# Up products of tile pairs by seven half-width products, with ScalarE's copies of sums into a second PSUM bank

## The chip, the cores and the metric

The kernel runs on one core of a Trainium2 chip. The metric is the device time of one execution in microseconds (us). The kernel before takes 976.99 us, the median of 3 runs (976.98 to 978.43).

## What is computed

One layer of a transformer on 512 positions of width 1024, all in fp32: a feed-forward block at half weight, a token mixer of two kinds of attention, a second feed-forward block at half weight and a last norm. The change touches the two feed-forward blocks alone:

```python
def swiglu(x, w_gate, w_up, w_down):
    return (jax.nn.silu(x @ w_gate) * (x @ w_up)) @ w_down

x = x + 0.5 * swiglu(rmsnorm(x, ffn1_norm), ffn1_w_gate, ffn1_w_up, ffn1_w_down)
```

`w_gate` and `w_up` are 1024 by 2816, that is 22 column tiles of 128; `w_down` is 2816 by 1024.

## The kernel before

Every fp32 product is three matmuls. An operand is split into a high part (ScalarE copies it to fp32r, lines 91, 188, 261) and a low part (VectorE subtracts, lines 92, 189, 262); `mm3` (lines 99 to 102) adds high times high, high times low and low times high into one PSUM bank. So each weight costs a cast on ScalarE and a subtraction on VectorE before TensorE can use it.

A feed-forward block (`ffn`, line 175) goes through the 22 tiles of gate and up columns, and then through the 8 output tiles of the down product. The first `n1` tiles (6 in the first block, "a", 4 in the second, "b") are plain: 8 blocks of the contraction, 512 positions wide. The others go in pairs (`pair`, line 250). The gate columns of a pair of tiles, eight blocks each way, are multiplied in Winograd's form of Strassen's scheme: seven products of half the contraction and 256 positions each, instead of eight. One such product is 4 blocks of 3 matmuls, 12 matmuls of 256 columns; a pair's gate has 84. The data side of the scheme (the sums `th`, `tl`) is made once a block by `normed_t`; the weight side is four sums on VectorE (lines 266, 267, 270, 273: `s1`, `s2`, `r1`, `s2` again) and seven splits named a11, w2, w1, w3, a12, a22, w4. The results are added together on VectorE and ScalarE as they come: `w` is a half of the tile `sq`, filled by a copy of the first product (line 296), to which the second is added (298); the adds of lines 301, 302, 306 and 309 finish the sums, and ScalarE takes Silu of them (304, 307, 310).

The up columns of a pair are done tile by tile in full width (`up`, line 316): 8 blocks of 3 matmuls of 512 columns, 24 a tile, 48 a pair, with one cast and one subtraction of 128x1024 for each tile's weights (lines 91, 92). Line 313 multiplies up by Silu of gate, and `activated` (lines 185 to 189) splits the result for the down product. The first pair of a block (tiles 6 and 7 in a, 4 and 5 in b) does its up products ahead of its gate products.

Buffers. Weights land in `raw` tiles of 512 KB, of which three exist, by SyncE's DMA queue (line 85); high and low parts (`wh`, `wl`) have three buffers each, `s1` and `s2` share two (`ob`), `g0` and `g1` two (`ptb`). A buffer is given to the next tile when the last reader of the one before is done. A gate set uses four high and four low tiles, each holding two splits side by side, in the order in which TensorE uses them up. PSUM has four banks for tag `mm` (the four accumulators pa, pb, pc, pd of a gate set, of which half is used), two for `s` and two for `t` (the up products).

Order of the work. TensorE's order in the feed-forward is that of the program. Those of ScalarE, VectorE and the DMA queue are set beforehand by a planner that goes through the program with its own estimate of each instruction's cost: on each engine the earliest instruction of the program among those that it thinks ready comes next. On the chip every engine then keeps this order, and waits for semaphores where something is not there yet.

In the profile the tiles have the block's letter: pwa, pxa, pya, pza are pa, pb, pc, pd of block a; `wh_sga` are high parts of gate weights, `wh_sua` of up weights, `wh_2a` and `wh_3a` the third and fourth high tile of a gate set; aha and ala are the split activations.

Of the kernel before, what the change touches and what calls it, by code (L numbers as in the profile page):

```python
# [13 lines left out]
F32 = mybir.dt.float32  # L14
F32R = mybir.dt.float32r
I32 = mybir.dt.int32
AF = mybir.ActivationFunctionType
ALU = mybir.AluOpType
AX = mybir.AxisListType

P = 128
S = 512
D = 1024
FF = 2816
KD = D // P
JF = FF // P
# [12 lines left out]

EARLY = (5, 3)  # L40
PAIRED = (6, 4)
HS = S // 2
F32_MAX = 3.4028234e38
PSUM = bass.MemoryType.PSUM
# [5 lines left out]
def tile_macaron(ctx: ExitStack, tc, xs, xT, wf, wgu1, wst1, wd1, wqk, wv, wo, wgu2, wst2, wd2,  # L50
                 lams, relb, onehot, addc, out):
    nc = tc.nc
    V, A, G, T = nc.vector, nc.scalar, nc.gpsimd, nc.tensor
# [4 lines left out]
    wp = ctx.enter_context(tc.tile_pool(name="wp", bufs=3))  # L58
    tp = ctx.enter_context(tc.tile_pool(name="tp", bufs=2))
    sp = ctx.enter_context(tc.tile_pool(name="sp", bufs=4))  # L60
    pp = ctx.enter_context(tc.tile_pool(name="pp", bufs=4, space=PSUM))
# [5 lines left out]
    def mm_bank(nm):  # L67
        return pp.tile([P, S], F32, tag="mm", name=nm, bufs=4)
# [5 lines left out]
    sq = cp.tile([P, S], F32, tag="sq", name="sq")  # L74
# [8 lines left out]
    def load_w(src, nm, n=1024):  # L83
        raw = wp.tile([P, 1024], F32, tag="raw", name=f"raw_{nm}")
        nc.sync.dma_start(raw[:, :n], src)
        h = wp.tile([P, 1024], F32R, tag="wh", name=f"wh_{nm}")
        l = wp.tile([P, 1024], F32R, tag="wl", name=f"wl_{nm}")
        return raw, h, l

    def split_w(raw, h, l, a, b):  # L90
        A.copy(h[:, a:b], raw[:, a:b])  # L91
        V.tensor_tensor(l[:, a:b], raw[:, a:b], h[:, a:b].bitcast(F32), op=ALU.subtract)  # L92

    def get_w(src, nm, n=1024):
        raw, h, l = load_w(src, nm, n)
        split_w(raw, h, l, 0, n)
        return h, l

    def mm3(po, wh, wl, mh, ml, first, last, on=False):
        T.matmul(po, wh, mh, start=first, stop=False, skip_group_check=on)  # L100
        T.matmul(po, wh, ml, start=False, stop=False, skip_group_check=on)  # L101
        T.matmul(po, wl, mh, start=False, stop=last, skip_group_check=on)  # L102
# [72 lines left out]
    def ffn(wgu, wst, wd, n0, n1, norm, early, res, nm, hooks, first=None, last_halves=None):  # L175
# [9 lines left out]
        def activated(j, t):  # L185
            h = ah[j] = slot(j, f"ah{nm}{j}", F32R)
            l = al[j] = slot(JF + j, f"al{nm}{j}", F32R)
            A.copy(h[:], t[:])
            V.tensor_tensor(l[:], t[:], h[:].bitcast(F32), op=ALU.subtract)
# [25 lines left out]
        def t_places():  # L215
            tp.tile([P, 8], F32, tag="odd", name=f"odd{nm}", bufs=1)
            rows = [tp.tile([P, 5 * HS], F32R, tag=f"pr{p % 2}", name=f"tt{nm}{p}")
                    for p in range(4)]
            more = tp.tile([P, 12 * HS], F32R, tag="tx", name=f"tx{nm}", bufs=1)
            tl.extend(t[:, :4 * HS] for t in rows)  # L220
            th.extend(more[:, 4 * p * HS:4 * (p + 1) * HS] for p in range(3))
            th.append([t[:, 4 * HS:] for t in rows])

        def normed_t(p):
# [3 lines left out]
            t0, t1 = nx[2 * p], nx[2 * p + 1]  # L228
            u0, u1 = slice(0, HS), slice(HS, S)
            V.tensor_tensor(t0[:, u0], t0[:, u1], t0[:, u0], op=ALU.subtract)  # L230
# [16 lines left out]
            c = slice(half * HS, (half + 1) * HS)  # L247
            return xh[k][:, c], xl[k][:, c]

        def pair(j):  # L250
            src = [wst[j + i - n1] for i in range(2)]
            ups = [up(j + i, src[i][1]) for i in range(2)] if j == n1 else []
            (r0, h0, l0), (r1, h1, l1) = [load_w(src[i][0], f"sg{nm}{j + i}") for i in range(2)]
            u0, u1 = slice(0, 512), slice(512, 1024)
            h2, l2, h3, l3 = [wp.tile([P, 1024], F32R, tag=t, name=f"{t}_{i}{nm}{j}")
                              for i in (2, 3) for t in ("wh", "wl")]
            s1 = tp.tile([P, S], F32, tag="ob", name=f"s1{nm}{j}")
            s2 = tp.tile([P, S], F32, tag="ob", name=f"s2{nm}{j}")

            def split(t, h, l):  # L260
                A.copy(h, t)
                V.tensor_tensor(l, t, h.bitcast(F32), op=ALU.subtract)
                return h, l

            a11 = split(r0[:, u0], h0[:, u0], l0[:, u0])
            V.tensor_tensor(s1[:], r1[:, u0], r1[:, u1], op=ALU.add)
            V.tensor_tensor(s2[:], s1[:], r0[:, u0], op=ALU.subtract)
            w2 = split(s2[:], h0[:, u1], l0[:, u1])
            w1 = split(s1[:], h1[:, u0], l1[:, u0])
            V.tensor_tensor(r1[:, u0], r0[:, u0], r1[:, u0], op=ALU.subtract)  # L270
            w3 = split(r1[:, u0], h1[:, u1], l1[:, u1])
            a12 = split(r0[:, u1], h2[:, u0], l2[:, u0])
            V.tensor_tensor(s2[:], r0[:, u1], s2[:], op=ALU.subtract)
            a22 = split(r1[:, u1], h2[:, u1], l2[:, u1])
            w4 = split(s2[:], h3[:, u0], l3[:, u0])

            pa, pb, pc, pd = [mm_bank(f"p{c}{nm}{j}")[:, :HS] for c in "wxyz"]

            def product(po, w, mv, first, last):
                for p in range(4):  # L280
                    o = slice(p * P, (p + 1) * P)
                    mm3(po, w[0][:, o], w[1][:, o], *mv(p), first and p == 0, last and p == 3, not first)

            def b(i, half):
                return lambda p: block(2 * p + i, half)

            def t(i):
                c = slice(i * HS, (i + 1) * HS)
                return lambda p: (th[p][i] if p == 3 else th[p][:, c], tl[p][:, c])

            g0 = tp.tile([P, S], F32, tag="ptb", name=f"g0{nm}{j}")
            g1 = tp.tile([P, S], F32, tag="ptb", name=f"g1{nm}{j}")
            w = sq[:, :HS] if (j // 2) % 2 else sq[:, HS:]
            left, right = slice(0, HS), slice(HS, S)
            product(pa, a11, b(0, 0), True, True)
            A.copy(w, pa)
            product(pb, w2, t(3), True, True)
            V.tensor_tensor(w, pb, w, op=ALU.add)
            product(pc, w1, t(0), True, True)
            product(pd, w3, t(1), True, True)  # L300
            V.tensor_tensor(g1[:, right], pd, w, op=ALU.add)
            V.tensor_tensor(g1[:, right], pc, g1[:, right], op=ALU.add)
            product(pa, a12, b(1, 0), False, True)
            A.activation(g0[:, left], pa, AF.Silu)
            product(pd, a22, t(2), False, True)
            V.tensor_tensor(g1[:, left], pd, w, op=ALU.add)
            A.activation(g1[:], g1[:], AF.Silu)
            product(pc, w4, b(1, 1), False, True)
            V.tensor_tensor(g0[:, right], pc, w, op=ALU.add)
            A.activation(g0[:, right], g0[:, right], AF.Silu)  # L310
            for i, g in enumerate((g0, g1)):
                pu = ups[i] if ups else up(j + i, src[i][1])
                V.tensor_tensor(g[:], pu[:], g[:], op=ALU.mult)
                activated(j + i, g)

        def up(j, src):
            wh, wl = get_w(src, f"su{nm}{j}")
            pu = pp.tile([P, S], F32, tag="t", name=f"pu{nm}{j}", bufs=2)
            for k in range(KD):
                o = slice(k * P, (k + 1) * P)  # L320
                mm3(pu[:], wh[:, o], wl[:, o], xh[k][:], xl[k][:], k == 0, k == KD - 1)
                prepared(j, k)
            return pu
# [15 lines left out]
        for j in range(j0, n1):  # L339
            mv = (eh, el) if j < n0 else (xh, xl)  # L340
            if j == 2 and first is not None:
                pg, pu = [pp.tile([P, S], F32, tag="t", name=f"p{c}{nm}2", bufs=2) for c in "gu"]
            else:
                pg = mm_bank(f"pg{nm}{j}")
                pu = mm_bank(f"pu{nm}{j}")
            for hf in range(2):
                wh, wl = get_w(wgu[j, hf], f"gu{nm}{j}_{hf}")
                for kk in range(4):
                    k = hf * 4 + kk
                    for c, pt in ((0, pg), (1, pu)):  # L350
                        o = kk * 256 + c * P
# [12 lines left out]
        for m in range(KD):  # L364
# [7 lines left out]
            po = mm_bank(f"pd{nm}{m}")  # L372
            for c0 in range(0, JF, 8):
                n = min(8, JF - c0)
                wh, wl = get_w(wd[m, :, c0 * P:(c0 + n) * P], f"d{nm}{m}_{c0}", n * P)
                for kk in range(n):
                    k = c0 + kk
                    o = kk * P
# [22 lines left out]
    with tc.manual_schedule(engines={mybir.EngineType.DVE, mybir.EngineType.Activation}):  # L401
        for t in range(4):
# [3 lines left out]
            for kk in range(2):  # L406
                k = 2 * t + kk
# [17 lines left out]
                for j in range(2):  # L425
                    for c in range(2):
                        o = kk * 512 + (2 * j + c) * P
# [31 lines left out]
    n1 = {}  # L459
    means, spread = rstd("n1", n1)  # L460

    means()
    for m in ffn(wgu1, wst1, wd1, EARLY[0], PAIRED[0], 0, early, n1, "a",
                 {(2, 2): spread, "down": bias_rows}, firsts):
# [476 lines left out]
    means, spread = rstd("n3", n3)  # L941
    for m in ffn(wgu2, wst2, wd2, EARLY[1], PAIRED[1], 2, early, n3, "b",
                 {(0, 4): means, (0, 7): spread}, last_halves=last_halves):
# [91 lines left out]
```

## Time and profile before

| | before |
|---|---|
| median of 3 runs | 976.99 us |
| the profiled execution's own time | 977.07 us |
| its span, first to last instruction | 974.8 us |
| TensorE busy with matmuls | 961.4 us (99%), 5394 matmuls |
| VectorE busy | 577.6 us (59%) |
| ScalarE busy | 426.0 us (44%) |
| weight loads (raw tiles) | 512 KB each, 3.5 to 3.8 us from issue to landing |
| block a: first pair's gate set starts, down product starts | 84.2 us, 240.9 us of the span |
| block b: down product starts | 842.1 us |

The page's first part is busy time by engine, its second the span in 40 slices, its fourth the chain of work that ended last. In a timeline line stand the start in us, the length in us, the engine, the line of the kernel, the operation, what it writes and reads, the shapes, how many instructions are merged, and in brackets how long the engine stood idle before and who released it. PEld is TensorE's loading of weights, DVE is VectorE, ACT is ScalarE, SPq is SyncE's DMA queue. A matmul's length in the timeline contains its way through the array, so that matmuls overlap; the spacing of their starts is what each costs.

### The profile page before, as it was taken

The numbers are of one execution on the slowest core, as the hardware profiler recorded it, in microseconds if no ns is written. First come the engines' busy times: TensorE is split into PE (matmuls) and PEld (weight loads), VectorE is DVE, ScalarE is ACT, GpSimd is POOL, SyncE is SP. The second block draws the span as 40 slices with busy tenths as digits, with TensorE's granted clock in tenths as the row PEclk, the third lists the DMA queues.
The fourth block names the chain that finished last, engine by engine and source line by source line (L and its number), as shares of the span: only waits on it lengthen the run. The fifth ranks groups of instructions, "written<-read, shape, count | busy, mean of one in ns | idle before, by whom it ended". The sixth has DMA issues, their size and how long they took to land.

```text
span 974.8 us, 13809 instructions
## 1 busy us (share of the span) xinstructions
PE 961.4 (99%) x5394; PEld 839.6 (86%) x5394; DVE 577.6 (59%) x1108; ACT 426.0 (44%) x787; POOL 32.4 (3%) x34
## 2 busy tenths in 40 slices
PE   9999999999999999999999999999999999999996
PEld 7789998888788888988989888889988899888886
DVE  7698767765232336668764546797677566422223
ACT  6455444434232335566756554454444344322230
POOL 0000000000010110000000003000000000000110
PEclk9999999999999999999999999999999999999998
DMA  7232423224333351444342204232332233433312
GB/s 253 66 114 67 130 91 118 95 87 130 98 97 84 96 160 62 130 119 120 88 112 85 76 32 130 65 108 73 118 114 87 87 101 117 119 98 84 96 58 87
DMA packets 32720, 98.71 MB, mean 101 GB/s; under 512 B 3776, under 2 KB 6080, under 8 KB 32656
## 3 DMA queue, kind: packets, MB, share of 16 engines
q1 hardware_dynamic: 32480, 97.55, 32.8%
q8 instruction: 42, 0.69, 0.3%
q0 software_dynamic: 176, 0.30, 0.1%
q14 instruction: 22, 0.18, 0.1%
HBM read 92.55 MB, written 2.14 MB: 97 GB/s over the span
## 4 chain that ended last, share of the span: by engine, by line
PE 94%; DVE 3%; ACT 1%; DMA 1%; issue 1%; DVEq 0%; POOL 0%; ACTq 0%; POOLq 0%
PE pda L100 4%; PE pub L100 4%; PE pub L101 4%; PE pda L102 4%; PE pda L101 4%; PE pub L102 4%; PE pua L100 4%; PE pua L101 4%; PE pua L102 4%; PE pdb L101 4%; PE pdb L100 4%; PE pdb L102 4%; PE po L704 2%; PE pwo L100 1%; PE pwo L101 1%; PE pwo L102 1%
## 5 line engine op out<-in xcount | busy, mean ns | idle before, releaser
L100 PE MATMUL pda<-aha,wh_da 128*128 128x512 f32 x176 | 68.6, 390 | 0.0
L102 PE MATMUL pda<-aha,wl_da 128*128 128x512 f32 x176 | 68.5, 389 | 0.0
L101 PE MATMUL pda<-ala,wh_da 128*128 128x512 f32 x176 | 68.5, 389 | 0.0
L92 DVE TENSOR_TENSOR wl_db<-raw_db,wh_db 128x1024 fp32r<-128x1024 f32 (+1 forms) x24 | 27.3, 1136 | 62.2 <-ACT wh_db L91 62.1
L92 DVE TENSOR_TENSOR wl_da<-raw_da,wh_da 128x1024 fp32r<-128x1024 f32 (+1 forms) x24 | 27.2, 1135 | 58.7 <-ACT wh_da L91 58.6
L91 ACT CAST wh_db<-raw_db 128x1024 fp32r<-128x1024 f32 (+1 forms) x24 | 23.6, 981 | 86.2 <-PE pdb L101 78.7
L91 ACT CAST wh_da<-raw_da 128x1024 fp32r<-128x1024 f32 (+1 forms) x24 | 23.5, 981 | 84.2 <-PE pda L101 55.5
L101 PE MATMUL pdb<-alb,wh_db 128*128 128x512 f32 x154 | 59.9, 389 | 0.0
L102 PE MATMUL pdb<-ahb,wl_db 128*128 128x512 f32 x154 | 59.9, 389 | 0.0
L100 PE MATMUL pdb<-ahb,wh_db 128*128 128x512 f32 x154 | 59.9, 389 | 0.0
L100 PE MATMUL pub<-xh,wh_sub 128*128 128x512 f32 x144 | 56.1, 390 | 0.0
L101 PE MATMUL pub<-xl,wh_sub 128*128 128x512 f32 x144 | 56.1, 390 | 0.0
L102 PE MATMUL pub<-xh,wl_sub 128*128 128x512 f32 x144 | 56.0, 389 | 0.0
L670 DVE CUSTOM_DVE_ANT_0 pr<-sc,strip 128x128 f32<-128x128 f32 (+3 forms) x64 | 30.8, 488 | 34.0 <-PE sc L668 33.6
L127 POOL TENSOR_TENSOR sq<-sq,sqt 128x512 f32<-128x512 f32 x20 | 28.7, 1435 | 661.8 <-ACT sqt L126 661.8
L100 PE MATMUL pua<-xh,wh_sua 128*128 128x512 f32 x128 | 49.9, 390 | 0.0
L101 PE MATMUL pua<-xl,wh_sua 128*128 128x512 f32 x128 | 49.9, 390 | 0.0
L102 PE MATMUL pua<-xh,wl_sua 128*128 128x512 f32 x128 | 49.8, 389 | 0.0
L673 ACT ACTIVATE pr<-pr,mx 128x128 f32<-128x128 f32 (+3 forms) x64 | 36.0, 563 | 30.8 <-DVE mx L670 29.7
L100 PEld LDWEIGHTS pda<-aha,wh_da 128*128 128x128 f32 x176 | 33.0, 188 | 7.3 <-ACT wh_da L91 0.5
L101 PEld LDWEIGHTS pda<-ala,wh_da 128*128 128x128 f32 x176 | 33.0, 188 | 6.9
L102 PEld LDWEIGHTS pda<-aha,wl_da 128*128 128x128 f32 x176 | 33.0, 188 | 6.9
(470 smaller groups left out, 2889.7 us busy)
## 6 DMA issues: line engine op xcount, KB each, us to landing
raw_sub<-wst_dram SPq DMA_DIRECT2D x18, 512.0 KB, 3.6
raw_sgb<-wst_dram SPq DMA_DIRECT2D x18, 512.0 KB, 3.7
raw_sua<-wst_dram SPq DMA_DIRECT2D x16, 512.0 KB, 3.5
raw_sga<-wst_dram SPq DMA_DIRECT2D x16, 512.0 KB, 3.8
raw_da<-wd_dram SPq DMA_DIRECT2D x16, 512.0 KB, 3.6
raw_qk<-wqk_dram SPq DMA_DIRECT2D x16, 512.0 KB, 3.6
raw_db<-wd_dram SPq DMA_DIRECT2D x16, 512.0 KB, 3.5
raw_gua<-wgu_dram SPq DMA_DIRECT2D x8, 512.0 KB, 3.6
```

The source lines that it names most:

```text
L91: A.copy(h[:, a:b], raw[:, a:b])
L92: V.tensor_tensor(l[:, a:b], raw[:, a:b], h[:, a:b].bitcast(F32), op=ALU.subtract)
L100: T.matmul(po, wh, mh, start=first, stop=False, skip_group_check=on)
L101: T.matmul(po, wh, ml, start=False, stop=False, skip_group_check=on)
L102: T.matmul(po, wl, mh, start=False, stop=last, skip_group_check=on)
L127: G.tensor_tensor(sq[:], sq[:], t[:], op=ALU.add)
L670: V.tensor_tensor_reduce(out=pi, in0=ps[:, :w], in1=st["b"][m][:, w - 1::-1], op0=ALU.add, op1=ALU.min, scale=1.0, scalar=3.0e38, accum_ou ...
L673: A.activation(pi, pi, AF.Exp, scale=-1.0, bias=st["mx"][:, m, i:i + 1], accum_out=st["ls"][:, m, i:i + 1])
L704: T.matmul(st["po3"][:, i, d0:d0 + dn], st["ptb", m, i][:, k * P:(k + 1) * P], vt[u // 4, k][:, fo + d0:fo + d0 + dn], start=k == 0, stop= ...
```

## The change

The gate's set of seven becomes a function, `seven`, that both gate and up use. Pairs from tile 8 on (`UP_PAIRS`; seven pairs in each block) do their up products by it too, after their gate products: 84 matmuls of 256 columns instead of 48 of 512. The accumulators of the up set are the four banks of tags `s` and `t`. The first pair of each block, and tiles 6 and 7 of block b, keep the full-width up products.

Inside `seven` the order of products is new (a11, w3, w2, a12, w1, a22, w4), the splits lie in the high and low tiles in that order, and sums that VectorE made are now made in PSUM: ScalarE copies the first product (pa) into bank pb, TensorE adds the third product onto it, ScalarE copies that sum into bank pc, and TensorE adds the fifth and at the end the seventh onto it. The second product (pd) is copied to SBUF (`p7`: a half of the norm's tile `bc` for the gate, a half of `sq` for up) and added by VectorE at two places. For up sets VectorE's last steps multiply by Silu of gate, in halves of 256.

The up weights' columns of all pair tiles are laid out on the host in the order that the gate's had (`block_tiles`), and `up` reads them accordingly.

```diff
@@ -39,6 +39,8 @@
 
 EARLY = (5, 3)
 PAIRED = (6, 4)
+
+UP_PAIRS = range(8, JF, 2)
 HS = S // 2
 F32_MAX = 3.4028234e38
 PSUM = bass.MemoryType.PSUM
@@ -247,15 +249,17 @@
             c = slice(half * HS, (half + 1) * HS)
             return xh[k][:, c], xl[k][:, c]
 
-        def pair(j):
-            src = [wst[j + i - n1] for i in range(2)]
-            ups = [up(j + i, src[i][1]) for i in range(2)] if j == n1 else []
-            (r0, h0, l0), (r1, h1, l1) = [load_w(src[i][0], f"sg{nm}{j + i}") for i in range(2)]
+        def seven(j, c, banks, p7):
+
+
+
+            (r0, h0, l0), (r1, h1, l1) = [load_w(wst[j + i - n1][c], f"s{c}{nm}{j + i}")
+                                          for i in range(2)]
             u0, u1 = slice(0, 512), slice(512, 1024)
-            h2, l2, h3, l3 = [wp.tile([P, 1024], F32R, tag=t, name=f"{t}_{i}{nm}{j}")
+            h2, l2, h3, l3 = [wp.tile([P, 1024], F32R, tag=t, name=f"{t}_{i}{c}{nm}{j}")
                               for i in (2, 3) for t in ("wh", "wl")]
-            s1 = tp.tile([P, S], F32, tag="ob", name=f"s1{nm}{j}")
-            s2 = tp.tile([P, S], F32, tag="ob", name=f"s2{nm}{j}")
+            s1 = tp.tile([P, S], F32, tag="ob", name=f"s1{c}{nm}{j}")
+            s2 = tp.tile([P, S], F32, tag="ob", name=f"s2{c}{nm}{j}")
 
             def split(t, h, l):
                 A.copy(h, t)
@@ -264,22 +268,20 @@
 
             a11 = split(r0[:, u0], h0[:, u0], l0[:, u0])
             V.tensor_tensor(s1[:], r1[:, u0], r1[:, u1], op=ALU.add)
+            V.tensor_tensor(r1[:, u0], r0[:, u0], r1[:, u0], op=ALU.subtract)
+            w3 = split(r1[:, u0], h0[:, u1], l0[:, u1])
             V.tensor_tensor(s2[:], s1[:], r0[:, u0], op=ALU.subtract)
-            w2 = split(s2[:], h0[:, u1], l0[:, u1])
-            w1 = split(s1[:], h1[:, u0], l1[:, u0])
-            V.tensor_tensor(r1[:, u0], r0[:, u0], r1[:, u0], op=ALU.subtract)
-            w3 = split(r1[:, u0], h1[:, u1], l1[:, u1])
-            a12 = split(r0[:, u1], h2[:, u0], l2[:, u0])
+            w2 = split(s2[:], h1[:, u0], l1[:, u0])
+            a12 = split(r0[:, u1], h1[:, u1], l1[:, u1])
+            w1 = split(s1[:], h2[:, u0], l2[:, u0])
+            a22 = split(r1[:, u1], h2[:, u1], l2[:, u1])
             V.tensor_tensor(s2[:], r0[:, u1], s2[:], op=ALU.subtract)
-            a22 = split(r1[:, u1], h2[:, u1], l2[:, u1])
             w4 = split(s2[:], h3[:, u0], l3[:, u0])
 
-            pa, pb, pc, pd = [mm_bank(f"p{c}{nm}{j}")[:, :HS] for c in "wxyz"]
-
-            def product(po, w, mv, first, last):
+            def product(po, w, mv, first=False):
                 for p in range(4):
                     o = slice(p * P, (p + 1) * P)
-                    mm3(po, w[0][:, o], w[1][:, o], *mv(p), first and p == 0, last and p == 3, not first)
+                    mm3(po, w[0][:, o], w[1][:, o], *mv(p), first and p == 0, p == 3, not first)
 
             def b(i, half):
                 return lambda p: block(2 * p + i, half)
@@ -288,36 +290,60 @@
                 c = slice(i * HS, (i + 1) * HS)
                 return lambda p: (th[p][i] if p == 3 else th[p][:, c], tl[p][:, c])
 
+            pa, pb, pc, pd = banks
+            product(pa, a11, b(0, 0), True)
+            A.copy(pb, pa)
+            product(pd, w3, t(1), True)
+            A.copy(p7, pd)
+            product(pb, w2, t(3))
+            A.copy(pc, pb)
+            product(pa, a12, b(1, 0))
+            yield pa
+            product(pc, w1, t(0))
+            yield pc
+            product(pb, a22, t(2))
+            yield pb
+            product(pc, w4, b(1, 1))
+            yield pc
+
+        def half_banks(tags, j):
+            return [pp.tile([P, S], F32, tag=t, name=f"p{c}{nm}{j}", bufs=4 if t == "mm" else 2)
+                    [:, :HS] for t, c in zip(tags, "wxyz")]
+
+        def pair(j):
+            ups = [up(j + i) for i in range(2)] if j == n1 else []
             g0 = tp.tile([P, S], F32, tag="ptb", name=f"g0{nm}{j}")
             g1 = tp.tile([P, S], F32, tag="ptb", name=f"g1{nm}{j}")
-            w = sq[:, :HS] if (j // 2) % 2 else sq[:, HS:]
             left, right = slice(0, HS), slice(HS, S)
-            product(pa, a11, b(0, 0), True, True)
-            A.copy(w, pa)
-            product(pb, w2, t(3), True, True)
-            V.tensor_tensor(w, pb, w, op=ALU.add)
-            product(pc, w1, t(0), True, True)
-            product(pd, w3, t(1), True, True)
-            V.tensor_tensor(g1[:, right], pd, w, op=ALU.add)
-            V.tensor_tensor(g1[:, right], pc, g1[:, right], op=ALU.add)
-            product(pa, a12, b(1, 0), False, True)
-            A.activation(g0[:, left], pa, AF.Silu)
-            product(pd, a22, t(2), False, True)
-            V.tensor_tensor(g1[:, left], pd, w, op=ALU.add)
+            p7 = res["bc"][:, left]
+            run = seven(j, 0, half_banks(("mm", "mm", "mm", "mm"), j), p7)
+            A.activation(g0[:, left], next(run), AF.Silu)
+            V.tensor_tensor(g1[:, right], next(run), p7, op=ALU.add)
+            V.tensor_tensor(g1[:, left], next(run), p7, op=ALU.add)
             A.activation(g1[:], g1[:], AF.Silu)
-            product(pc, w4, b(1, 1), False, True)
-            V.tensor_tensor(g0[:, right], pc, w, op=ALU.add)
-            A.activation(g0[:, right], g0[:, right], AF.Silu)
+            A.activation(g0[:, right], next(run), AF.Silu)
+            if j in UP_PAIRS:
+                p7 = sq[:, left]
+                run = seven(j, 1, half_banks(("s", "t", "t", "s"), f"u{j}"), p7)
+                V.tensor_tensor(g0[:, left], next(run), g0[:, left], op=ALU.mult)
+                V.tensor_tensor(sq[:, right], next(run), p7, op=ALU.add)
+                V.tensor_tensor(sq[:, left], next(run), p7, op=ALU.add)
+                V.tensor_tensor(g1[:], sq[:], g1[:], op=ALU.mult)
+                V.tensor_tensor(g0[:, right], next(run), g0[:, right], op=ALU.mult)
+                activated(j + 1, g1)
+                activated(j, g0)
+                return
             for i, g in enumerate((g0, g1)):
-                pu = ups[i] if ups else up(j + i, src[i][1])
+                pu = ups[i] if ups else up(j + i)
                 V.tensor_tensor(g[:], pu[:], g[:], op=ALU.mult)
                 activated(j + i, g)
 
-        def up(j, src):
-            wh, wl = get_w(src, f"su{nm}{j}")
+        def up(j):
+            wh, wl = get_w(wst[j - n1][1], f"su{nm}{j}")
             pu = pp.tile([P, S], F32, tag="t", name=f"pu{nm}{j}", bufs=2)
             for k in range(KD):
-                o = slice(k * P, (k + 1) * P)
+                o = k // 2 * P + k % 2 * 4 * P
+                o = slice(o, o + P)
                 mm3(pu[:], wh[:, o], wl[:, o], xh[k][:], xl[k][:], k == 0, k == KD - 1)
                 prepared(j, k)
             return pu
@@ -988,9 +1014,9 @@
 
     def block_tiles(g, u, n):
 
-        g, u = [col_tiles(t)[n:].reshape(JF - n, P, KD, P) for t in (g, u)]
-        g = np.concatenate([g[:, :, 0::2], g[:, :, 1::2]], axis=2)
-        return np.ascontiguousarray(np.stack([g, u], axis=1)).reshape(JF - n, 2, P, KD * P)
+        t = np.stack([col_tiles(w)[n:].reshape(JF - n, P, KD, P) for w in (g, u)], axis=1)
+        t = np.concatenate([t[:, :, :, 0::2], t[:, :, :, 1::2]], axis=3)
+        return np.ascontiguousarray(t).reshape(JF - n, 2, P, KD * P)
 
     wi = a(w_in[0])
     qa, ka, va, qb, kb, vb = [wi[:, i * 512:(i + 1) * 512] for i in range(6)]
```

## The prediction

> **What bounds the kernel now.** I read the page first: busy shares, then the slices, then the chain of work that ended last.
>
> ```profile
> PE 961.4 (99%) x5394; PEld 839.6 (86%) x5394; DVE 577.6 (59%) x1108; ACT 426.0 (44%) x787; POOL 32.4 (3%) x34
> ...
> PEclk9999999999999999999999999999999999999998
> ...
> PE 94%; DVE 3%; ACT 1%; DMA 1%; issue 1%; DVEq 0%; POOL 0%; ACTq 0%; POOLq 0%
> ```
>
> TensorE is busy in every slice at its full granted clock, and the chain is TensorE's own. So the time is the sum of matmul spacings plus what TensorE waits. Next I cut one pair (tiles 12 and 13 of the first feed-forward) out with the windows view: its up products come first, then its gate products.
>
> ```profile
> 146.49:157.40 10.91, 10.91 (x51) 9.02 (x49) 7.66 (x12) 3.48 (x8) 0.00 (x0) 1.00 0.26 83
> 157.40:167.36 9.96, 9.96 (x85) 9.96 (x84) 6.37 (x11) 5.40 (x9) 0.00 (x0) 1.00 0.41 118
> 146.49:167.36 20.87, 20.87 (x134) 18.98 (x133) 14.04 (x23) 8.88 (x16) 0.00 (x0) 1.00 0.33 100
> ```
>
> After the length stand the busy times of PE, PEld, DVE, ACT and POOL. 48 up matmuls of 512 columns take 10.91 us, 0.227 each; 84 gate matmuls of 256 take 9.96 us, 0.1186 each. TensorE has no gap in either. (Windows share an edge with their neighbours, hence 51 and 85.) Within the gate window DVE is idle 3.6 us and ACT 4.6.
>
> The last view is the only place in each feed-forward where one gate set of seven follows another without 10.9 us of full-width products between them: the first pair, whose up products ran earlier. It is the nearest row to what every pair becomes. Timeline, first feed-forward:
>
> ```profile
> 85.76 0.33 SPq L85 DMA_DIRECT2D raw_sga<-wst_dram  x1
> ...
> 89.41 0.69 DVE L266 TENSOR_TENSOR s1a<-raw_sga 128x512 f32<-128x512 f32 x1 [0.72 <-DMA raw_sga<-wst_dram]
> 90.13 0.69 DVE L267 TENSOR_TENSOR s2a<-s1a,raw_sga 128x512 f32<-128x512 f32 x1
> ...
> 90.74 0.68 DVE L270 TENSOR_TENSOR raw_sga<-raw_sga,raw_sga 128x512 f32<-128x512 f32 x1
> ...
> 91.34 0.42 DVE L301 TENSOR_TENSOR g1a<-pza,sq 128x256 f32<-128x256 f32 x1
> 91.35 0.28 PE L102 MATMUL pwa<-xh,wl_2a 128*128 128x256 f32 x1
> ...
> 91.81 0.39 PE L100 MATMUL pza<-txa,wh_2a 128*128 128x256 f32 x1 [0.19 <-DVE g1a L301]
> ...
> 92.04 0.28 PE L101 MATMUL pza<-tta,wh_2a 128*128 128x256 f32 x1
> ```
>
> A raw tile was free at 85.73, 1.5 us into the set (it began at 84.20). Its reload landed at 89.39, 3.65 later. DVE stood 0.72 us for it, then did three sums, with the add that TensorE needed behind them. TensorE lost 91.81-91.47 = 0.34 us, and 0.11 more because the first matmul after the wait takes 0.23 instead of 0.12: **0.45 us**. The same place in the second feed-forward (671.60 to 672.18, then 672.40) gives 0.56.
>
> **The change, part by part.**
>
> Matmuls. In 14 pairs (tiles 8 to 21, twice) 48 full matmuls become 84 half ones: 10.91 - 9.96 = 0.95 us, times 14 = **-13.3 us**, all of it on the path. That the spacing stays 0.1186 is the gate row's. The Trainium skill, TensorE: Matmul & The Clock Gate, Back-to-back issue gap, says that weight loads share in setting the spacing, 81 ns at 128 columns and 131 at 512. A straight line between gives 98 at 256, an estimate, 0.75 of a full one; by it the up products would take 14.3 us, 3.4 more a pair, and the kernel 48 more. The row says 0.52 and decides.
>
> DVE, per pair, by start-to-start spacing in the timeline (0.60 for 128x512, 0.34 for 128x256, 1.14 for 128x1024). Splits: seven at 0.60 for two at 1.14, +1.92. Four sums of weights, +2.40. Ends: five adds and two full products (2.90) become six of 256 and one full (2.64), -0.26. Sum +4.06, so busy 14.04 becomes 18.1 of the 19.92 us that the matmuls leave: 91%.
>
> ACT, per pair: seven casts at 0.52 for two at 0.95, +1.74; six copies of 128x256 for one, at 0.37 (the row of line 296), +1.85. 8.88 becomes 12.5 of 19.92. Both lie beside TensorE so long as nothing is late. Loads keep their bytes and number.
>
> Hand-over between sets. 26 new places (13 in each feed-forward) have one set right behind another, with three raw buffers for two tiles a set. I count from a set's start. Ahead of the last read that frees a raw tile, DVE now has mul g1 0.60, mul g0 0.34, four subtractions of splits (w2, a12, w1, a22) and the two of the activations: about 4.5 us of issue, with 0.7 until the last one lands 5.0 to 5.2. The reload lands at 8.8; s1 0.72, r1 0.72, w3's cast 0.65 and its subtraction 0.72 bring 11.6. TensorE wants w3 as the second product of the next set: 9.96 + 1.42, and its low part two matmuls later: 11.6. So it arrives just in time if DVE has nothing else between; an add at 0.34 and a sum at 0.60 do fall there. Bounds: 0, and 0.94. I take the row, (0.45+0.56)/2 = 0.505 each: **+13.1 us**. What is late here first is DVE's place in order, not the DMA.
>
> Copies into a second bank. TensorE now waits for ScalarE: product three adds onto a copy of product one, product five onto a copy of product three. A product is 12 x 0.1186 = 1.42; the last matmul ends 0.16 after the next product starts, the copy is 0.37, so 0.84 is left for ScalarE's queue. What stands ahead of the copy in it:
>
> ```profile
> 157.37 1.14 ACT L261 CAST wh_2a<-raw_sga 128x512 fp32r<-128x512 f32 x2 [3.72 <-PE pua L101]
> 158.42 0.61 ACT L188 CAST aha<-g1a 128x512 fp32r<-128x512 f32 x1
> 159.03 0.37 ACT L296 COPY sq<-pwa 128x256 f32<-128x256 f32 x1
> ```
>
> The set began at 157.40, its first product ended at 158.98: three casts ahead and still on time. Now w2, w1, a22 and both activation casts start near a set's start: five at 0.52 from 0.2 end at 2.8, the copy at 3.2, against 2.85: 0.35 late and 0.11 of restart. Behind the copy stand the next casts of the set, wanted four products later. Bounds: 0 and 0.46 a set. I take 0.1, near the row's end: 28 x 0.1 = **+2.8 us**. No row shows ScalarE writing a bank; between 0.30 (a 256 cast's spacing) and 0.6 it stays inside these bounds. The wait of product seven for DVE's read of its bank has the same 0.8 of slack and is in the hand-over's price.
>
> Sum: -13.3 + 13.1 + 2.8 = +2.6. The profiled execution took 977.07 (span 974.8 and 2.27 around it), 0.08 over the median of 976.99. Forecast 977.07 + 2.6 = **979.7 us**.
>
> **The rivals.**
>
> *Hand-overs hidden.* If the instruction order spreads DVE's work so that reloads come earlier, 0.1 stays of each: -13.3 + 2.6 = -10.7, 966.4. For it: steady pairs have no TensorE gap today, and in the new order only two adds of the gate remain. Against it: 0.45 and 0.56 in both rows, with less DVE work than now.
>
> *DVE becomes the bound (slower).* The place is DVE's queue in every pair from tile 8. Idle forced on it by operands that land late adds to 18.1 us; from 20.87 - 18.1 = 2.8 us a pair the change loses. The first pair's 12.8 us (84.20 to 97.00) had DVE busy 9.89: 2.9 idle, 4.5 in 19.92, which would make 22.6 a pair and +24 us, the far end, 1001. Some of that idle closes up under load; with 3.5 a pair is 21.6, +10.5, and 988. For it: the 91%. Against it: DVE idles before splits that are not urgent.
>
> *Weight loads set the pace.* 84 x 0.188 (PEld's mean) = 15.8 for 10.91, +68: 1045. Against it: the gate window holds 84 loads in 9.96 us. The rule of the skill above points this way.
>
> *The change does not do what it says:* the up sets come out of the order so late that pairs last as before, 977. Against it: no instruction but those counted stands between.
>
> **How the numbers follow.** A measurement can tell about 0.2%, 1.95 us. Forecast mechanism 0.50: its hand-over between 0.3 and 0.75 and its copies spread it over 974 to 987: 0.05 faster, 0.19 within, 0.26 slower. Hidden 0.22, faster. DVE bound 0.25, slower. Weight loads 0.01, slower. Not as said 0.02, within. Together 0.27 faster, 0.21 within, 0.52 slower. The range goes from 967, which leaves out half of the hidden case, to 990, which leaves out the worse part of the DVE case; 973 to 987 is the forecast's own.
>
> **What would show it.** Steady pairs of 20.5 to 21.5 us from one a11 to the next; TensorE idle before w3's or product seven's matmuls in about every second set with DVE named, and a few tenths before product three with ACT named; 84 matmuls in 9.96 us plus such gaps; DVE over 80% in the pair stage. A pair at 19.9 to 20.1 without gaps makes me wrong to the fast side, one over 21.6 with DVE never idle to the slow side; a spacing above 0.12 inside a product would break the first term.

## The result, and the profile after

The changed kernel takes 983.45 us (median of 4 runs, 981.67 to 983.67), the kernel before 977.12 us on the same chip (976.98 to 978.43): the ratio is 1.006, 95% interval 1.0044 to 1.0076. It is slower by 0.6%, as forecast in sign; the forecast was 979.7 us.

The two profiled executions stand at 981.67 and 977.07 us, +4.6, and both at a mean granted clock of 0.997. The other three runs of the changed kernel had 0.996 and spans of 981.0 to 981.4 us against 979.4. So some 1.7 us of the 6.3 between the medians come with runs at a lower clock (the last section shows what such a run can look like), and the traces have to explain 4.6.

The page after, busy times and the chain that ended last:

```profile
PE 955.5 (98%) x5898; PEld 855.1 (87%) x5898; DVE 625.7 (64%) x1225; ACT 472.6 (48%) x933; POOL 32.4 (3%) x34
...
PE 79%; DMA 7%; DVE 7%; ACT 4%; issue 2%; DVEq 0%; SPq 0%; ACTq 0%
```

TensorE has less work than before (961.4), and the chain, which was 94% TensorE, now passes through transfers, VectorE and ScalarE for 18% of the span. The windows view, two steady pairs of the first block, each from a gate set's product three to the next pair's (length, then busy PE, PEld, DVE, ACT, POOL, granted clock, DMA share, GB/s):

```profile
118.67:140.12 21.45, 20.49 (x168) 20.11 (x168) 17.57 (x32) 12.10 (x26) 0.00 (x0) 1.00 0.28 99
140.12:161.46 21.34, 20.44 (x169) 20.07 (x169) 17.58 (x32) 12.09 (x26) 0.00 (x0) 1.00 0.28 99
```

A pair took 20.87 us before, would take 168 x 0.1186 = 19.92 without a wait, and takes 21.4. Where this 1.4 to 1.5 goes is seen in TensorE's timeline of one pair, of which these are the first matmuls of the gate's product three (into pxa) and product seven (into pya), the only two places with a wait:

```profile
140.12 0.39 PE L102 MATMUL pxa<-txa,wh_s0a 128*128 128x256 f32 x1
140.35 0.28 PE L103 MATMUL pxa<-tta,wh_s0a 128*128 128x256 f32 x1
...
146.90 0.35 PE L102 MATMUL pya<-xh,wh_30a 128*128 128x256 f32 x1 [0.83 <-DVE g1a L321]
```

Product three starts 0.25 late, and the matmul behind it comes 0.23 later instead of 0.12; these 0.11 are called the restart below. Product seven starts 0.99 late, with a restart of 0.07. Adding up, over both blocks' pairs, what each start spacing has over 0.1186 (0.227 for 512 columns): 12.53 us at the gate's product seven, 3.87 at the gate's product three, 1.86 in the up sets (at their product seven), 18.26 in all. Before the change it was 1.01, in the two first pairs. So -13.3 + 18.26 - 1.01 = +3.95, against +4.60 measured. In the pair stages, from the first gate matmul of the pairs to the first of the down product, block a takes 3.11 us more than before and block b 1.06, and the rest of the kernel 0.40; so most of the missing 0.65 lies outside the pairs, and its cause is not shown.

What product seven waits for is in VectorE's timeline ahead of it:

```profile
141.41 0.68 DVE L266 TENSOR_TENSOR wl_20a<-raw_s0a,wh_20a 128x512 fp32r<-128x512 f32 x1
142.02 0.68 DVE L278 TENSOR_TENSOR s20a<-raw_s0a,s20a 128x512 f32<-128x512 f32 x1
143.44 0.69 DVE L266 TENSOR_TENSOR wl_30a<-s20a,wh_30a 128x512 fp32r<-128x512 f32 x1 [0.74 <-ACT wh_30a L265]
144.05 0.69 DVE L266 TENSOR_TENSOR wl_s1a<-raw_s1a,wh_s1a 128x512 fp32r<-128x512 f32 x1
145.73 0.69 DVE L270 TENSOR_TENSOR s11a<-raw_s1a 128x512 f32<-128x512 f32 x1 [0.99 <-DMA raw_s1a<-wst_dram]
146.33 0.42 DVE L321 TENSOR_TENSOR g1a<-pya,rbc_n 128x256 f32<-128x256 f32 x1
```

Read from the end. The add at 146.33 reads bank pya, into which product seven must accumulate; its operand was there at about 144.66, when product five's last matmul (144.38, 0.28 long) was through. But in VectorE's order the up set's first sum (s11a) stands ahead of it, and that sum stands 0.99 us for its raw tile's transfer. The transfer in turn was issued at 142.16, 5.2 us into the set, which began at 137.00, right behind the end of the read at 141.41 (142.09), the second last that VectorE makes of the gate set's raw tiles. TensorE pays for a sum that it needs only one set later.

What product three waits for is in ScalarE's timeline:

```profile
138.67 0.61 ACT L190 CAST aha<-g1a 128x512 fp32r<-128x512 f32 x1
139.19 0.62 ACT L190 CAST aha<-g0a 128x512 fp32r<-128x512 f32 x1
139.71 0.36 ACT L295 COPY pxa<-pwa 128x256 f32<-128x256 f32 x1
```

Product one's last matmul was through at 138.61; the copy of it starts 1.1 later, behind the casts of the pair before. In the up sets no activation casts stand there, and the copy is in time.

### The profile page after: what moved, and what is told of

It is laid out like the page before. It is cut to its first block, busy times and chain, and to the rows that moved or that the text cites. A ratio compares the mean times of both kernels' runs of the same rounds, so it can differ in the third digit from the quotient of the medians.

```text
span 979.4 us, 15122 instructions
## 1 busy us (share of the span) xinstructions
PE 955.5 (98%) x5898; PEld 855.1 (87%) x5898; DVE 625.7 (64%) x1225; ACT 472.6 (48%) x933; POOL 32.4 (3%) x34
## 4 chain that ended last, share of the span: by engine, by line
PE 79%; DMA 7%; DVE 7%; ACT 4%; issue 2%; DVEq 0%; SPq 0%; ACTq 0%
PE pda L102 4%; PE pda L104 4%; PE pda L103 4%; PE pdb L102 4%; PE pdb L103 4%; PE pdb L104 4%; DMA raw_s1a<-wst_dram 3%; PE po L730 2%; DMA raw_s0a<-wst_dram 2%; DMA raw_s1b<-wst_dram 2%; PE pub L102 1%; PE pub L103 1%; PE pub L104 1%; PE pua L103 1%; PE pua L102 1%
## 5 line engine op out<-in xcount | busy, mean ns | idle before, releaser
L730 PEld LDWEIGHTS po<-v,ptb 128*128 128x128 f32 x240 | 32.7, 191 | 4.9 <-ACT ptb L720 2.3
L588 PE MATMUL pv<-wh_v,xh 128*128 128x256 f32 x128 | 36.2, 283 | 0.0
L590 PE MATMUL pv<-wl_v,xh 128*128 128x256 f32 x128 | 36.2, 283 | 0.0
L589 PE MATMUL pv<-wh_v,xl 128*128 128x256 f32 x128 | 36.2, 283 | 0.0
L104 PEld LDWEIGHTS pdb<-ahb,wl_db 128*128 128x128 f32 x154 | 28.9, 188 | 6.1
L102 PEld LDWEIGHTS pdb<-ahb,wh_db 128*128 128x128 f32 x154 | 28.9, 188 | 6.0
```

What stands on the lines that cost most here:

```text
L588: T.matmul(po, xh[k][:, xs], wh[:, o:o + 256], start=k == 0, stop=False)
L589: T.matmul(po, xl[k][:, xs], wh[:, o:o + 256], start=False, stop=False)
L590: T.matmul(po, xh[k][:, xs], wl[:, o:o + 256], start=False, stop=k == KD - 1)
L730: T.matmul(st["po3"][:, i, d0:d0 + dn], st["ptb", m, i][:, k * P:(k + 1) * P], vt[u // 4, k][:, fo + d0:fo + d0 + dn], start=k == 0, stop= ...
```

## The experiments

In the diffs `...` stands for lines left out. The theory to test, called ORDER: TensorE loses where VectorE's fixed order puts something that waits for a late reload ahead of an add that frees a bank. Its rivals: VECTORE (its work, 17.6 us of each pair, sets the pair's length), RELOAD or FREEING (the weights come too late whatever the order), COPY (ScalarE's queue). Every time below is a median, beside that of the kernel before, measured with it (977.2 to 978.2 us).

### The add ahead of the next set's first sum

```diff
-            V.tensor_tensor(s1[:], r1[:, u0], r1[:, u1], op=ALU.add)
+            with tc.issue_after(after) if after is not None else ExitStack():
+                V.tensor_tensor(s1[:], r1[:, u0], r1[:, u1], op=ALU.add)
...
```

`after` is the add of line 321 (for a gate set, that of line 329 of the up set before); `issue_after` fixes the order on the engine and adds no wait.

> VectorE's first sum of every set of seven (s1, which waits for the second raw tile's reload) is queued behind the add that reads product five's bank for the set before; nothing else changes. ORDER theory (the reload makes s1 wait, and the add stands behind s1 only because VectorE's order has it there): the 11 waits of 1.0 to 1.2 us before the gate's product seven go, 12.5 us in all, and the profiled 981.7 us of the changed kernel becomes 968 to 972. VECTORE theory (its 18 us of work in each pair set the pair's length): the idle only moves to another place, 980 to 984, with new waits of about 1 us before the up set's second product. RELOAD theory (the weights themselves come too late, whatever the order): product seven's wait goes but the up set's products that need the late tile wait 0.4 to 0.7 us instead, 974 to 978.

Measured: 975.24 us, ratio to before 0.9978 (0.9969 to 0.9987), 8.2 below the changed kernel. VectorE's timeline, with the reload still late but nothing right behind it that TensorE needs at once:

```profile
143.22 0.42 DVE L324 TENSOR_TENSOR g1a<-pya,rbc_n 128x256 f32<-128x256 f32 x1
144.41 0.69 DVE L271 TENSOR_TENSOR s11a<-raw_s1a 128x512 f32<-128x512 f32 x1 [0.77 <-DMA raw_s1a<-wst_dram]
```

The waits at product seven fall from 12.53 us to 0.05, as ORDER says. But at least 3 us less were won than expected: the up set's product three now waits 0.3 to 0.47 us in 12 places, 6.29 in all with the restarts, for ScalarE's copy, which stands behind casts of the sums that came late. The RELOAD theory's loss exists too, and shows once the other wait is gone.

### The activations behind the copy

```diff
-            A.copy(pb, pa)
+            copied = A.copy(pb, pa).ins
+            if late:
+                with tc.issue_after(copied):
+                    while late:
+                        activated(*late.pop(0))
...
```

`late` holds the pair's two tiles, whose `activated` is thus put off into the next gate set.

> The two activation casts and subtractions of a pair are put behind ScalarE's copy of product one's sum into the second bank of the next gate set. COPY theory (the wait before the gate's product three is ScalarE's queue alone): 13 waits of 0.15 to 0.26 with a restart of 0.11 each, 3.9 us in all, go, and the changed kernel's 981.7 becomes 977 to 979. SLACK theory (the pair's length is held by VectorE and the reload behind it): product three starts earlier, but product seven then waits longer by as much, 981 to 983.

Measured: 973.33 us (0.9957, 0.9942 to 0.9972), better than either theory gave. The waits at product three go (3.87 to 0.54, what is left is in each block's second gate set), but those at product seven fall too, to 2.42. The edit moved two operations of VectorE as well: the activations' subtractions now come behind the reads that free the raw tiles, so the reload comes earlier (in the pair shown, in the same order, the sum 7.47 us after its set's start instead of 8.73). The sum's wait was 0.99 and is 0.29:

```profile
143.19 0.69 DVE L270 TENSOR_TENSOR s11a<-raw_s1a 128x512 f32<-128x512 f32 x1 [0.29 <-DMA raw_s1a<-wst_dram]
143.80 0.42 DVE L327 TENSOR_TENSOR g1a<-pya,rbc_n 128x256 f32<-128x256 f32 x1
```

One loss grew: the up set's product seven waits in 12 places and loses 5.8 us with restarts, where the changed kernel loses 1.86. It waits for the add of line 329 in the changed kernel, which stands behind the next gate set's first sum; that is the same order one set later.

### Raw tiles in halves

```diff
+            self.t = [wp.tile([P, 512], F32, tag="raw", name=f"raw{i}_{nm}", bufs=6)
+                      for i in range(2)]
...
+        for a in range(0, n, 512):
+            b = min(n, a + 512)
+            nc.sync.dma_start(raw[:, a:b], src[:, a:b])
...
```

> Raw tiles are kept as two halves of 512 columns, six of them in the same memory, each loaded by a transfer of its own; so the left halves come free and are loaded again some 3 us earlier. Casts and subtractions of the other stages, too, are made in halves. ORDER and RELOAD theories: VectorE no longer stands about 1 us for the reload, the 11 waits before the gate's product seven shrink below 0.3 us, 968 to 973. VECTORE theory: its work is unchanged in the pairs, 980 to 984.

Measured: 968.29 us (0.9911, 0.9894 to 0.9927), in the range of ORDER and RELOAD. The sum comes 4.39 us after its set's start and does not wait:

```profile
139.47 0.68 DVE L282 TENSOR_TENSOR s11a<-raw_s1a,raw_s1a 128x512 f32<-128x512 f32 x1
...
143.32 0.42 DVE L333 TENSOR_TENSOR g1a<-pya,rbc_n 128x256 f32<-128x256 f32 x1
```

Product seven keeps a wait of 0.17 with 0.10 of restart in 13 places: five operations stand between the sum and the add. So the late reload and the order are both needed for the loss at product seven, and taking away either is a cure for it. The waits at the gate's product three fall to 0.55 here too, with no cast moved by hand, which suggests that ScalarE's queue was late in part because the sums that it casts were late; no run holds the two apart.

### The gate's new order alone

```diff
-UP_PAIRS = range(8, JF, 2)
+UP_PAIRS = ()
```

> The list of pairs whose up products are made by seven half-width products is empty; what is left of the change is the gate's new order of products, ScalarE's copies into a second bank and the new column order of the up weights. If the new order of the gate costs nothing by itself: 976 to 978, as before the change. If the copies' waits belong to it and not to the up sets: 0.3 us in each of 15 gate sets, 980 to 983.

Measured: 978.46 us (1.0011, 1.0002 to 1.0021), just above the first case: +1.05 us, of which the trace has 0.93 as small waits (1.94 in all, against 1.01 before). The gate's new order costs 1 us; the other 5 of the changed kernel are what the up sets cost beyond the matmuls that they save.

### VectorE's subtractions late, and left out

Two edits on its side alone: the activations' two subtractions put behind the last read of the raw tiles, and the same two not made at all, which leaves out part of the computation (the high parts stand in for the low ones in the down product).

```diff
-            V.tensor_tensor(s2[:], r0[:, u1], s2[:], op=ALU.subtract)
+            last = V.tensor_tensor(s2[:], r0[:, u1], s2[:], op=ALU.subtract).ins
+            with tc.issue_after(last):
+                low_parts()
...
```

```diff
+            if j >= 8:
+                al[j] = h
+                A.copy(h[:], t[:])
+                return
```

> VectorE's two low-part subtractions of a pair's activations (0.60 us each) are queued behind the last read that frees a raw tile in the next set; ScalarE's casts stay where they were. FREEING theory (what was won by putting the activations behind the copy came mostly from VectorE's side: the raw tiles come free 1.2 us earlier, so the reload lands earlier and the sum ahead of the gate's add no longer waits): the waits before product seven fall to 0.2 or less, those before the gate's product three (0.36 each with restart) stay, 973 to 977. COPY theory (it came from ScalarE's queue): both kinds of waits stay, 980 to 984.

> Leaves out part of the computation: the low parts of the activations of tiles 8 to 21 are not computed, and the high part stands in their place in the products of the down projection. VectorE has 1.2 us less work a pair, and the raw tiles come free 1.2 us earlier as in the run with these subtractions late. FREEING theory: as that run within 1.5 us. VECTORE theory (its total work sets the length): 3 us or more below it, since 1.2 us in each of 14 pairs go out of a chain that is full.

Measured: 981.98 us (1.0048, 1.0031 to 1.0065) and 981.95 us (1.0047, 1.0031 to 1.0063), nearly the changed kernel's. The FREEING expectation failed for the first; that the second takes as long as the first is as it said. The raw tiles do come free earlier, and in the pair shown the sum comes 6.61 and 6.42 us after its set's start instead of 8.73. But the planner, which sees the sum earlier too, now puts four operations of the up set, counted from the sum, ahead of the add instead of one (three in most pairs). VectorE with the subtractions late:

```profile
144.58 0.69 DVE L280 TENSOR_TENSOR s11a<-raw_s1a 128x512 f32<-128x512 f32 x1 [1.52 <-DMA raw_s1a<-wst_dram]
145.31 0.69 DVE L281 TENSOR_TENSOR raw_s1a<-raw_s1a,raw_s1a 128x512 f32<-128x512 f32 x1
145.92 0.68 DVE L276 TENSOR_TENSOR wl_s1a<-raw_s1a,wh_s1a 128x512 fp32r<-128x512 f32 x1
146.52 0.69 DVE L283 TENSOR_TENSOR s21a<-s11a,raw_s1a 128x512 f32<-128x512 f32 x1
147.12 0.42 DVE L333 TENSOR_TENSOR g1a<-pya,rbc_n 128x256 f32<-128x256 f32 x1
```

So the gate's product seven still loses 10.5 and 8.8 us. Two other losses moved against each other, which COPY, whose 980 to 984 us held, did not expect: the gate's product three falls from 3.87 to 0.9 in both, and the up set's product seven grows from 1.86 to 6.4 and 6.3, behind the next gate set's sum.

The run without the subtractions settles the VECTORE theory: 1.2 us of VectorE's work less in each of 14 pairs, 16.8 in all, and the time falls by 1.5 (by 2.3 in the pair stages of the traces). VectorE only waits longer for the same transfer, 14.0 us in seven places where the changed kernel had 6.8 in its waits view:

```profile
DVE s11a L274 <- DMA raw_s1a<-wst_dram: 14.0, 7, 2.8
```

### The add later still

The up set's loads and sums are made ahead of the gate's last steps in the program, and the add is held behind the up set's difference:

```diff
+                run_u = seven(j, 1, lambda: half_banks(("s", "t", "t", "s"), f"u{j}"), sq[:, left])
+                with tc.issue_after(next(run_u)):
+                    V.tensor_tensor(g1[:, right], after, p7, op=ALU.add)
...
```

> The opposite of moving the add ahead: the gate's add that frees product five's bank is queued behind the up set's first sum, its difference and its second sum (three operations of 0.60 us, where the changed kernel has the first alone ahead of the add). ORDER theory (each operation behind the late reload and ahead of the add is paid by TensorE): the wait before the gate's product seven grows from 1.1 by 1.2 to about 2.3 us in 11 to 13 places, 994 to 998. Against it (the wait is for the transfer or for VectorE's total work, and its inner order matters little): 981 to 986.

Measured: 991.62 us (1.014, 1.0125 to 1.0156), 8.2 more than the changed kernel. The direction is ORDER's, the size was expected larger. PE's waits:

```profile
PE pya L102 <- DVE g1a L327: 9.3, 7, 1.5
PE pyb L102 <- DVE g1b L327: 7.6, 6, 1.5
```

In the changed kernel this view has 5.2 and 4.4 in eleven places, at most 1.1 each; now 13 wait, up to 1.5, and with restarts product seven loses 20.4 us instead of 12.53. The 1.2 us of two more operations are not paid in full, since the sum itself comes 0.6 earlier in its set (8.13). The copies' waits moved from product three to product five, 5.19 us.

### Both orders, and what each brings

The first two edits together:

> Both changes of order together: the add that frees product five's bank ahead of the next set's first sum, and the activations behind the copy. If the two waits are separate, what is left is about 4 us of TensorE's waits in the pairs, 967 to 970. If the up set's product three again waits for ScalarE's copy behind the casts of late sums, as with the add alone (0.45 us with 0.10 of restart in 11 places), 972 to 974.

Measured: 966.14 us (0.9882, 0.9864 to 0.99), below the first case. One steady pair and the place that waited:

```profile
136.76:156.74 19.98, 19.98 (x169) 19.98 (x169) 17.77 (x32) 12.04 (x26) 0.00 (x0) 1.00 0.30 106
```

```profile
142.27 0.42 DVE L330 TENSOR_TENSOR g1a<-pya,rbc_n 128x256 f32<-128x256 f32 x1
142.61 0.68 DVE L271 TENSOR_TENSOR s11a<-raw_s1a 128x512 f32<-128x512 f32 x1
```

TensorE is busy throughout; its waits in the pairs are 1.78 us in all. A pair lasts 19.98 us, 0.89 less than before the change.

The add ahead, with the subtractions late and ScalarE's casts as they were:

> The gate's add is held ahead of the up set's first sum, and the activations' subtractions are behind the last read that frees a raw tile; ScalarE's casts are not moved by hand. Beside the run with the add alone (975.2) it shows what the 1.2 us of earlier freeing bring, and beside the run with both changes of order (966.1) what ScalarE's order brings. FREEING theory: the up set's waits at product three (0.55 with restart in 11 places) go with the earlier reload, those at the gate's product three (0.3 in 13) stay: 968 to 971. COPY theory (ScalarE's order did it all): 974 to 976.

Measured: 968.4 us (0.9904, 0.9889 to 0.9918), as FREEING says. Once the add's place is fixed, the earlier freeing is worth 6.8 us (975.24 to 968.4), since the planner can no longer spend it ahead of the add. ScalarE's order is the last 2.3 us between the medians and 3.3 in the pair stages of the traces: the gate's product three keeps 4.04 us of waits here and 0.55 in the version with both.

On top of both orders, each subtraction of the activations made twice:

```diff
+            for _ in range(2 if j >= 8 else 1):
...
```

> The version with both changes of order, and each of VectorE's low-part subtractions of the activations of tiles 8 to 21 made twice: 1.2 us more of its work in each of 14 pairs, 18.8 of about 20.0 us. ORDER theory (VectorE's total is not the bound): 965 to 969. VECTORE theory: about 1.2 us a pair, 980 to 984.

Measured: 968.91 us (0.9912, 0.9897 to 0.9927), at the upper end of what ORDER gave. The 1.2 us more in each pair cost 0.2 in the medians (0.25 in the pair stages of the traces):

```profile
136.80:157.13 20.33, 20.33 (x169) 20.10 (x169) 18.71 (x34) 12.19 (x26) 0.00 (x0) 1.00 0.30 104
```

VectorE at 18.71 of 20.33 us is not the bound yet, but its slack is nearly gone: small waits appear at product seven and in the up set's second product, 5.51 us in all.

The halves of raw tiles with the add ahead, and with both orders. In these two only the up set's first sum is held behind the gate's add; the gate set's is left to the planner:

> Half raw tiles, and the gate's add ahead of the up set's first sum. With the reload early, the 13 waits of 0.17 with 0.10 of restart before the gate's product seven that were left go, 3.5 us: 964.5 to 966. If moving the sum behind the add makes the up set's sums late (a wait at its product three as with the add alone): 967 to 970.

> Both changes of order and the half raw tiles together. With the two changes of order alone TensorE's waits in the pairs are 1.5 us in all, so the earlier reloads have almost nothing left to win: 965 to 967, the same as without them. Faster than 964 would mean a wait that the trace does not show.

Measured: 966.67 us (0.9891, 0.9871 to 0.9911) and 966.09 us (0.9883, 0.9866 to 0.9899). The first is a little over its range, the second in it; neither is to be told from 966.14. Early reloads have nothing left to win once the order is right; waits of 2.1 and 1.4 us stay at the up set's product seven, most of them at one place. The version with both orders is 17.3 us below the changed kernel and 11 below the kernel before (the ratio above), with the same operations and buffers as the changed kernel.

## Why the prediction was right, and where it was not

**The sign and the bound** held: TensorE's matmuls became fewer, and waits between sets took more than they saved.

**Matmuls, -13.3.** Right. The steady pair of the version with both orders lasts 19.98 us, 0.05 of it a wait, so 0.94 less than 20.87; 168 matmuls keep 0.1186. The estimate from the figures of the Trainium skill (TensorE: Matmul & The Clock Gate, Back-to-back issue gap), by which the change would have cost 48 us more, is not borne out: 168 weight loads fit into these 19.98 us.

**VectorE and ScalarE, 18.1 and 12.5 us a pair.** 17.6 and 12.1 measured. That VectorE at this load is no bound by itself is shown from both sides, by 1.2 us less a pair in the changed kernel (-1.5 us in all) and 1.2 us more in the version with both orders (+2.8).

**Hand-over, 26 places at 0.505, +13.1.** The mechanism was right, and so, by luck, was the sum: 12.53 at the gate's product seven and 1.86 in the up sets. The count and the price were not. The row that gave 0.505 was read as a price for every hand-over; in truth 11 of the 14 from gate to up cost 1.0 to 1.3 each with the restart, and those from up to gate little. The sentence that put w3's arrival just in time was right (no wait at w3 anywhere), and it was the add for product seven that decided. Its wait was put "in the hand-over's price", without asking what stands ahead of that add in VectorE's order. That is a sum whose operand was 0.99 us late. From up to gate the same order stands, but there the sum mostly starts 6.6 to 7.2 us after its set's start, against about 8.7, and the add behind it is in time.

**"What is late here first is DVE's place in order, not the DMA."** Half right. Moving the add cures the wait at product seven with the transfer as late as before; an earlier transfer, by half tiles, cures most of it with the sum still ahead of the add. It takes both.

**Copies into a second bank, 28 at 0.1, +2.8.** This is the step that was mis-sized in kind: 0.30 a place in 13 gate sets (3.87), next to nothing in the up sets. The working beside it had 0.35 late and 0.11 of restart from five casts in the queue, and the trace shows 0.25 and 0.11 behind such casts. The value was then taken near the row of the old kernel, in which the queue was shorter. The working knew better than the row.

**What was left out.** The 1.01 us of the kernel before's own stalls, which the new sets replace, and runs at a lower clock, which put 1.7 us between the medians that the traces do not have. By the trace's account the change costs +3.95 where +2.6 was forecast.

**The rivals.** *Hand-overs hidden* gave 966.4, and the version with both orders takes 966.1: its 2.6 us of waits were 1.78, its condition (that the planned order would bring this by itself) was not met. *VectorE as the bound* came out with a time near the measured one (988 against 983). Its operands that land late in VectorE's queue are what the runs found; that VectorE's work and this idle add up to the pair's length they exclude, since with 1.2 us less work the idle grew (14.0 for 6.8 us) and with the same work in another order the pair took 19.98. *Weight loads* did not come, and neither did pairs as long as before.

**The signs named** came: most steady pairs last 21.0 to 21.6 us, TensorE stands before the gate's product seven with DVE named, in every second set, and a few tenths before product three for ScalarE's copy, and DVE is busy 82% of a pair. Three figures of the prediction are off by its own terms: the slack of 0.84 us for ScalarE's queue is 0.89 (1.42 - 0.16 - 0.37), the +10.5 of VectorE as the bound is 10.2, and the first pair's gate set began at 84.36 us, not at 84.20. None of them changes the forecast.

## What to carry to other kernels

Where one engine works ahead for the next stage, look at its order, not only at its load: an operation that waits for a transfer holds up all that stands behind it, and the price is paid by whoever waits for the last of these. After a change that shortens a stage, list for each short product what must be read or copied before its bank may be used again, and which late operand stands ahead of that read in its engine's queue. Two edits that only fix an order were worth 17 us here, and an operand that came 2 us earlier was worth next to nothing (1.5 us) where the planner put more work ahead of the read that mattered.

## What the runs showed of the hardware

The granted clock sets runs of one kernel apart by some 1.5 us. In all 14 traces it is full from about 7 us on, up to the last 5.6 to 9.3 us of the span, which are at half clock. Six of them have one stretch more at half clock, 3.41 us long, between 551 and 564 us, in the token mixer, which the change does not touch. In the version with both orders it is here (3.40 us, TensorE busy throughout, granted clock 0.51):

```profile
551.80:555.20 3.40, 3.40 (x11) 2.80 (x10) 1.68 (x7) 0.92 (x4) 0.00 (x0) 0.51 0.45 130
```

Matmuls of 512 columns start 0.42 to 0.43 us apart in it, against 0.227, and the time from block a's down product to block b's first up product is 369.7 us in these six traces, 368.1 to 368.2 in the eight others. The mean over the run shows it only as 0.993 to 0.995 where the best runs have 0.997, and a longer end at half clock lowers the mean as well. Of the other runs no trace was kept, so what lowered their clock is not shown: the kernel before, in the 19 runs beside the first experiments, had spans of 974.4 to 974.8 us at 0.997 and 975.1 to 977.8 at 0.995. The pair stages lie outside these stretches, and for differences below 2 us they are the better measure: 334.06 us before, 338.23 after the change and 321.63 with both orders, the two blocks together.

ScalarE's copy of 128x256 from one PSUM bank into another lasted 0.357 to 0.376 us (medians of lines 295 and 299, gate and up sets), and 0.372 to 0.373 from PSUM to SBUF (line 297). The Trainium skill (ScalarE: Activation LUTs, Step-by-step: what each stage is for) says that ScalarE writes PSUM faster than SBUF. At this size that is 0.016 us at most in this trace, and at line 295 of the up sets it is 0.003 the other way.
